# Accumulating DMAs for all weight sums, one norm step for four heads, and two K-parts in the first output projection

## The chip, the cores and the metric

The kernel runs on one core of a Trainium2 chip and computes two model blocks in one program. The metric is device time in microseconds; the time before is 1748.75 us, the median of three runs (1745.6 to 1749.56).

## The reference

512 tokens and 16 meta tokens (L = 528 rows) of width 2048 go through two blocks, all in float32. Cut to what matters:

```python
# block 1
hn   = rmsnorm(h, pre_norm_g)
proj = hn @ w_in                       # 2048 -> qa, ka, va, ga | qb, kb, vb, gb
ya   = softmax(rope(rms(q)) @ rope(rms(k)).T / sqrt(128)) @ v      # 8 heads "A", 2 kv heads
ya  *= silu(ga)
a    = softmax(q1 @ k1.T / 8 - slope*dist) - lam * softmax(q2 @ k2.T / 8 - slope*dist)
yb   = rms(a @ vb) * (1 - lambda_init) * silu(gb)                  # 8 heads "B"
h    = h + rmsnorm(concat(ya, yb) @ w_out, post_norm_g)
# block 2 (512 tokens): stick-breaking attention and a gated linear recurrence,
# each gated by silu, concatenated, projected by w_out_2 and added to h
```

## The kernel before, in words

Every float32 product is made of three TensorE passes on float32r halves (`PASSES`): a tile is cast by ScalarE to a high half and VectorE subtracts it to get the low half (`split`, lines 167 to 169). Weights come by SyncE DMAs into `wraw`, and are split into `wsp`.

Matmuls are queued on TensorE in an order that the program fixes while it is written. `run` (line 226) holds one main generator (the projections) and many side generators (the attention heads), and keeps a clock, `state["clock"]`, that adds an estimated cost for each matmul. A step that needs the result of other engines waits for a key; `post(key, ns)` (line 208) makes that key ready `ns + 300` after the clock. A side step whose keys are ready is queued ahead of the main work, and where the main generator itself waits for a key, side steps follow one another with no main work between them. What is fixed there is only the order: on the chip each matmul starts when its semaphores allow.

Block 1 goes in this order on TensorE. First K and V of attention A and its queries. Then 20 **pairs** (`PAIRS`: four pairs of gates of A, four of gates of B, then for every two B heads a Q/K pair, a V pair and a Q/K pair). A pair computes two 128-column tiles of the projection; 12 of its 16 K tiles go through `seven` (line 428), seven products of sums of weight halves with sums of input halves in place of eight, the other four K tiles through `rest`. The products are queued as 1, 4, 5, rest 6, 3, rest 6, 2, 7, rest 8, rest 8, 9; each product is 18 matmuls. The raw halves r0 to r3 of a pair are 128 x 768. `produce(p, i)` (line 356) splits the weight of product i and starts the next sum: r0 becomes w0+w1 by a VectorE add (line 373), then +w2 and +w3 by GpSimd DMAs that accumulate into SBUF (`sum_up`, line 352), and r1 becomes w1+w2 by another such DMA. GpSimd also does half of the rope of attention A (line 663), the bias table of a B head (line 882) and one step of its norm (line 964), in one queue with these DMAs.

The side steps of attention: `a_scores` (line 806) normalizes one A query head (a Square, a reduction, `rsqrt` with 12 small VectorE instructions, rope), transposes it and queues four score groups; `a_sums`/`pv_steps` (line 693) transpose the probabilities (two groups of four transposes into the one PSUM tile `ptt`, lines 705 to 711), split them into `pt` and multiply by V (`pmt`, 13 matmuls). `b_scores` (line 878) queues eight score groups of a B head through the one PSUM tile `pss`, each read by the fused add-and-minimum of line 912; `b_sums` (line 934) does its values and norm. The Q/K pair of head h may only empty product 5's bank into `qs_` when the head before it has been taken up (key `qkused`, line 1266), and the first V pair when attention A is done (key `suma`, line 1292).

After the pairs comes the first output projection O1: 512-column strips n, each summed over four K groups kg of 512; kg 3 needs the last four B heads. Strip 0 is summed over kg 0 to 2 and copied to SBUF (`to_part`), strip 1 over kg 0 to 3, then strip 0 gets kg 3; strips 2 and 3 follow by token pairs. Weights of O1 may only be loaded when `barred` is raised (line 1314), after the last pair.

Of the kernel before, what the change touches and what calls it, by code (L numbers as in the profile page):

```python
# [16 lines left out]
P = 128  # L17
# [77 lines left out]
def _sequence():  # L95


    seq = [("VA", 0)] + [("QA0", kg) for kg in range(4)] + [("QA1", kg) for kg in range(4)] + [("VA", 1)]
    seq += [("O1", 0, kg) for kg in range(3)] + [("O1", 1, kg) for kg in range(4)] + [("O1", 0, 3)]
    seq += [("O1", n, kg) for _ in range(2) for n in (2, 3) for kg in range(4)]  # L100
    seq += [("XL", b) for _ in range(2) for b in range(8)]
    seq += [("GL", b) for b in range(8)] + [("GS", b) for b in range(8)]
    for c in range(4):
        if c % 2 == 0:
            seq += [("v", c // 2, kg) for kg in range(4)]
        seq += [("qk", c, kg) for kg in (QK_LAST if c == 3 else range(4))]
    seq += [("O2", n, kg) for n in range(4) for kg in (0, 2, 3)] + [("O2", n, 1) for n in range(4)]
    return [(("KA", i), h) for h in range(2) for i in range(2)] + [(u, h) for u in seq for h in range(2)]
# [3 lines left out]
def hybrid_two_block_kernel(ctx: ExitStack, tc: tile.TileContext, wp, wq, wc, xT, xtok, par, lvec, cst, rg, pg, lruw, out):  # L112
# [92 lines left out]

    HOP = 300.0

    def post(key, ns=0.0):
        ready[key] = state["clock"] + (ns + HOP if ns else 0.0)

    def hold(key):
        ready[key] = math.inf
# [139 lines left out]
    def sum_up(p, r, q):  # L352

        pool.dma_start(pair_raw[(p, r)], wq[p, q], accum_op=ALU.add)  # L354

    def produce(p, i):


        if p >= len(PAIRS):
            return  # L360
        r = lambda k: pair_raw[(p, k)]
        if i == 1:
            pair_w[(p, "at")] = dict(zip("abcd", w_slots))
        at = pair_w[(p, "at")]
        src, place = {1: (0, "a"), 2: (0, "b"), 4: (1, "c"), 5: (3, "d"), 6: (4, "a"), 3: (0, "c"), 8: (5, "d"),
                      7: (2, "c"), 9: (0, "b")}[i]
        n = NCL * P if i in (6, 8) else WS
        slot = at[place]
        w = halves(wsp_all[:, 2 * WS * slot : 2 * WS * slot + 2 * n])
        pair_w[(p, i)] = w  # L370
        split(w[:, 0], w[:, 1], r(src))
        if i == 1:
            dve.tensor_tensor(r(0), r(0), r(1), ALU.add)
            sum_up(p, 1, 2)
        elif i == 2:
            sum_up(p, 0, 2)
        elif i == 3:
            sum_up(p, 0, 3)
        elif i == 4:
            load_raw(p, 4, raw_slot[(p, 1)])  # L380
        elif i == 5:
            load_raw(p, 5, raw_slot[(p, 3)])
        elif i == 6:
            w_slots[:] = [at["a"], at["c"], at["d"], at["b"]]
            load_raw(p + 1, 0, raw_slot[(p, 4)])
        elif i == 8:
            load_raw(p + 1, 1, raw_slot[(p, 5)])
        elif i == 7:
            load_raw(p + 1, 2, raw_slot[(p, 2)])
        elif i == 9:  # L390
            load_raw(p + 1, 3, raw_slot[(p, 0)])
# [36 lines left out]
    def seven(p, r, c0a, c0b, evac_a1, evac_b, evac_a2, after=None):  # L428
# [43 lines left out]
        if p == 0:  # L472
            yield when("x4")
        yield from product(7, 1, lambda xs, j: big[:, xs, j, HL + c0b : L], slice(c0b, HL), True, False)
        produce(p + 1, 2)
        if after:
            after()
        yield from rest(8, 2, 0, False, True, True)
        yield from rest(8, 1, c0b, True, False, True)
        yield from evac_b()  # L480
        produce(p + 1, 4)
        yield from product(9, 3, lambda xs, j: big[:, xs, KS + j, X2], allc, False, True)
        yield from evac_a2()
        produce(p + 1, 5)
# [248 lines left out]
    va = [None, None]  # L733
    lnload = [None, None]
    kb_ = [None]

    def side_norms():
        ready[("start", -1)] = 14000.0
# [67 lines left out]
    def a_scores(h, e):  # L806
        g = h // 4
        yield when(("qa", g), *([("feat", h - 1)] if h else []))
        x = qraw[:, :, (h % 4) * P : (h % 4 + 1) * P]
        act.activation(blocks(at1), x, AF.Square)  # L810
        ssq = small(4)
        dve.tensor_reduce(ssq, blocks(at1), axis=AX.X, op=ALU.add)
        rope(x, rsqrt(ssq, 4, 1.0 / P), 4, cq, sq_, at1, au)
        post(("pq", h), 14000)
        if h % 4 == 3:
            post(("qaused", g))
        yield when(("pq", h), "pmt", ("kt", 0), ("kt", 1), *([("scored", h - 2)] if h > 1 else []))
        tb = pmt()
        for t in range(NT):
            tr(tb[:, t * P : (t + 1) * P], at1[:, t * P : (t + 1) * P], ident)  # L820
        qh = T([P, 2, 512], "qq", F32R, 2)
        split(qh[:, 0], qh[:, 1], tb)
        post("pmt", 2400)
        post(("feat", h))
        post(("q", h), 3600)
        for qt in range(4):
            yield when(("q", h), "pss", 1)
            take_e(1)
            s = pst()
            qs = slice(qt * P, (qt + 1) * P)  # L830
            for pi, (a, b) in enumerate(PASSES):
                for c in range(2):
                    mm(s[:, c, :HL], qh[:, a, qs], kt_[0][:, g, b, c * HL : (c + 1) * HL], pi == 0, pi == 2)
            nm, l = small(1), small(2)
            sv = s[:, :, :HL]
            dve.tensor_reduce(nm, sv, axis=AX.XY, op=ALU.max, negate=True)  # L836
            x = et()
            act.activation(halves(x), sv, AF.Exp, bias=nm, accum_out=l[:, 0:1])  # L838
# [327 lines left out]
    def main_work():  # L1166
# [31 lines left out]
        def last_x2k1(kt):  # L1198
            if kt == KS - 1:
                post("x2k1")  # L1200
            elif kt == 11:
                for r in range(4):
                    load_raw(0, r, r)
                produce(0, 1)
                produce(0, 4)

# [2 lines left out]
        produce(0, 5)  # L1209
        yield when("xs")  # L1210
        banks = [pjt() for _ in range(4)]
        r0, r1, r2_, r3 = banks
        HR = HL - NM
        pair_no = {pair: i for i, pair in enumerate(PAIRS)}
# [48 lines left out]
        def qkb(h):  # L1263
# [14 lines left out]
                return ()  # L1278

            def after():  # L1280
                for kt in range(KS):
                    split_ready(kt)

# [32 lines left out]
        part = [ar[:, c : c + 512] for c in (2560, 4608, 5120, 5632)]  # L1316

        def o1_evac(n, from_part=False):
            c = slice(n * 512, (n + 1) * 512)

            def evac(accs):
                yield when("pgb")
                for t in accs:
                    y = accs[t]
                    if from_part:
                        y = part[t]
# [6 lines left out]
        def to_part(accs):  # L1333
            yield when(("vused", 7), ("qkused", 7))
            for t in accs:
                act.copy(part[t], accs[t])

        def o1(n, kgs, evac, toks=range(NT)):
            def slots(kg):
# [244 lines left out]
```

## Time and profile before

| | |
|---|---|
| median of 3 runs | 1748.75 us |
| the profiled execution: its own time | 1746.56 us |
| its span, first to last instruction | 1744.8 us |
| matmuls on TensorE | 10288, busy for 1691.8 us |
| VectorE, ScalarE, GpSimd busy | 1131.7, 899.3, 135.8 us |
| pairs 0 to 8, at 157 to 429 us | gates of A and B, first Q/K pair, attention A beside them |
| pairs 9 to 19, at 429 to 738 us | Q, K and V of B, attention B beside them |
| O1, from 738 us | with the last B heads up to 850 us |

In the tables of stretches, each row gives the length of a stretch, then the busy time of TensorE (PE), of its weight loads (PEld), VectorE (DVE), ScalarE (ACT) and GpSimd (POOL) with their instructions, the clock granted to TensorE as a share of full speed (PEclk), and the DMA load. In a row of waits stand the waiting instruction, what released it, the total, the times and the longest. In a timeline row stand the start and the length in microseconds, engine, line, operation, tiles and shapes, and in brackets the idle time of the engine just before it. SPq and POOLq are the DMA queues of SyncE and GpSimd.

### The profile page before, as it was taken

Reading aid. Unit: us, or ns where it says so; the run is one execution under the profiler, and the core shown is the slowest. Engines: PE = TensorE matmul, PEld = TensorE weight load, DVE = VectorE, ACT = ScalarE, POOL = GpSimd, SP = SyncE. Lnnn points to the kernel's source line nnn. Section 1 sums busy time; section 2 is a strip of 40 time slices with the busy share of each in tenths; the row PEclk is TensorE's granted clock in tenths of the full one; section 3 lists DMA queues with packets and bytes.
Section 4 is the critical chain, followed back from the end, with each engine's and each line's share of the span. In section 5 each row is a group of like instructions: output and inputs, shape, how many; then the busy total and the mean of one; then the engine's idle time right before and its main releaser. Section 6 shows DMA issues by size and latency. Waiting matters only on the chain.

```text
span 1744.8 us, 26494 instructions
## 1 busy us (share of the span) xinstructions
PE 1691.8 (97%) x10288; PEld 1504.6 (86%) x10288; DVE 1131.7 (65%) x1947; ACT 899.3 (52%) x1489; POOL 135.8 (8%) x145
## 2 busy tenths in 40 slices
PE   8999998999999998999799999999999999999998
PEld 8789988999999998978588998888888888888887
DVE  5775778877788888875458868843223564585433
ACT  6454555665566676665345548832222654565311
POOL 0101111110112111110000001100000000000000
PEclk9999999999999999999899999999999999999999
DMA  8444754656645554543368664223332222432223
GB/s 301 156 132 128 181 131 116 156 142 156 145 116 130 124 136 105 151 138 94 106 217 273 211 198 129 83 97 97 97 97 93 77 73 85 138 116 85 85 90 127
DMA packets 82668, 231.70 MB, mean 133 GB/s; under 512 B 9312, under 2 KB 15072, under 8 KB 80864
## 3 DMA queue, kind: packets, MB, share of 16 engines
q1 hardware_dynamic: 73904, 206.43, 36.9%
q0 software_dynamic: 8640, 23.60, 8.6%
q8 instruction: 80, 1.31, 0.3%
q14 instruction: 44, 0.36, 0.1%
HBM read 212.17 MB, written 17.83 MB: 132 GB/s over the span
## 4 chain that ended last, share of the span: by engine, by line
PE 77%; DVE 4%; DMA 1%; ACT 1%; issue 1%; POOL 0%; SPq 0%; ACTq 0%; DVEq 0%; POOLq 0%
PE pj L201 67%; PE pmt L201 3%; PE pss L201 3%; PE ptt L204 2%; PE bank L201 1%; DVE wsp L169 1%; PE pmt L204 1%; PE pss L204 1%; DVE e L912 0%; DMA wraw<-in_wc 0%; DMA yd<-xmisc 0%; DVE ar L960 0%; ACT wsp L168 0%; DVE pt L169 0%; DMA wraw<-in_wp 0%
## 5 line engine op out<-in xcount | busy, mean ns | idle before, releaser
L201 PE MATMUL pj<-wsp,big 128*128 128x512 f32 x3072 | 739.4, 397 | 16.5 <-ACT big L168 10.4
L201 PEld LDWEIGHTS pj<-wsp,big 128*128 128x128 f32 x3072 | 572.7, 189 | 145.5 <-ACT big L168 10.8
L201 PE MATMUL pj<-big,wsp 128*128 128x264 f32 (+3 forms) x4320 | 636.7, 304 | 9.3 <-ACT big L543 5.6
L201 PEld LDWEIGHTS pj<-big,wsp 128*128 128x128 f32 x4320 | 582.8, 189 | 46.4 <-ACT big L543 5.9
L169 DVE TENSOR_TENSOR wsp<-wraw,wsp 128x1024 fp32r<-128x1024 f32 (+3 forms) x399 | 425.0, 1068 | 300.5 <-ACT wsp L168 294.9
L168 ACT CAST wsp<-wraw 128x1024 fp32r<-128x1024 f32 (+3 forms) x399 | 366.4, 922 | 412.9 <-PE pj L201 330.2
L201 PE MATMUL pj<-x,wsp 128*128 128x264 f32 x720 | 102.1, 288 | 0.2 <-DVE wsp L169 0.2
L201 PEld LDWEIGHTS pj<-x,wsp 128*128 128x128 f32 x720 | 93.6, 190 | 0.6 <-DVE wsp L169 0.4
L354 POOL DMA_DIRECT2D wraw<-in_wq x60 | 52.7, 879 | 381.1 <-DVE wsp L169 154.9
L169 DVE TENSOR_TENSOR pt<-ptt,pt 128x512 fp32r<-128x512 f32 (+2 forms) x96 | 59.5, 619 | 30.8 <-ACT pt L168 29.5
L201 PE MATMUL pss<-kk,qq 128*128 128x264 f32 x448 | 73.7, 293 | 4.3 <-DVE sm L912 3.8
L201 PE MATMUL pmt<-pt,vv 128*128 128x256 f32 (+1 forms) x528 | 72.4, 287 | 4.9 <-DVE ptail L716 3.2
L201 PEld LDWEIGHTS pmt<-pt,vv 128*128 128x128 f32 x528 | 69.7, 196 | 7.8 <-issue 3.3
L915 ACT ACTIVATE e<-e,sm 128x528 f32<-128x528 f32 x64 | 47.2, 737 | 52.7 <-DVE sm L912 52.0
L168 ACT CAST pt<-ptt 128x512 fp32r<-128x512 f32 (+2 forms) x96 | 50.2, 523 | 40.8 <-PE ptt L204 40.5
L201 PEld LDWEIGHTS pss<-kk,qq 128*128 128x128 f32 x448 | 63.4, 193 | 7.3 <-DVE sm L912 4.6
L204 PE MATMUL ptt<-ident,e 128*128 128x128 f32 x336 | 53.2, 275 | 10.3 <-DVE pt L169 10.3
L912 DVE CUSTOM_DVE_ANT_0 e<-pss,ar 128x528 f32<-128x528 f32 x64 | 45.0, 703 | 18.4 <-PE pss L201 18.0
L204 PEld LDWEIGHTS ptt<-ident,e 128*128 128x128 f32 x336 | 40.0, 141 | 14.7 <-DVE pt L169 8.6
L201 PE MATMUL pj<-x1s,wsp 128*128 128x264 f32 x360 | 50.8, 287 | 0.0
L1120 POOL TENSOR_SCALAR_AFFINE_SELECT e<-e 128x128 f32<-128x128 f32 x32 | 12.7, 395 | 479.2 <-ACT e L1119 473.2
L838 ACT ACTIVATE e<-pss,sm 128x528 f32<-128x528 f32 x32 | 22.5, 702 | 48.3 <-DVE sm L836 48.2
(249 smaller groups left out, 1438.1 us busy)
## 6 DMA issues: line engine op xcount, KB each, us to landing
wraw<-in_wp SPq DMA_DIRECT2D x215, 512.0 KB, 3.5
wraw<-in_wq SPq DMA_DIRECT2D x80, 384.0 KB, 3.4
wraw<-in_wq POOLq DMA_DIRECT2D x60, 384.0 KB, 5.0
wraw<-in_wc SPq DMA_DIRECT2D x40, 256.0 KB, 2.7
e<-in_xT SPq DMA_DIRECT2D x28, 264.0 KB, 4.4
early<-in_xtok SPq DMA_DIRECT2D x4, 1024.0 KB, 7.2
gated<-e SPq DMA_DIRECT2D x16, 256.0 KB, 2.3
e<-yd SPq DMA_DIRECT2D x16, 256.0 KB, 3.8
```

The costliest lines, as they stand in the source:

```text
L168: act.copy(hi, src)
L169: dve.tensor_tensor(lo, src, f(hi), ALU.subtract)
L201: _queue(nc.tensor.matmul(out, lhsT, rhs, start=start, stop=stop).ins, cost)
L204: _queue(nc.tensor.transpose(out, in_, identity).ins, 110.0)
L354: pool.dma_start(pair_raw[(p, r)], wq[p, q], accum_op=ALU.add)
L838: act.activation(halves(x), sv, AF.Exp, bias=nm, accum_out=l[:, 0:1])
L912: dve.tensor_tensor_reduce(out=halves(x), in0=s[:, :, :HL], in1=halves(bias[:, b0 : b0 + L]), scale=1.0, scalar=3e38, op0=ALU.add, op1=ALU ...
L915: act.activation(x, x, AF.Exp, scale=-1.0, bias=nm, accum_out=l[:, m : m + 1])
L1120: pool.affine_select(z[:, t * P : w], z[:, t * P : w], [[-1, P]], ALU.is_gt, -1e30, base=0, channel_multiplier=1)
```

## The change

Five things are edited.

- **Weight sums.** r0 + w1 is now a DMA too (`sum_up(p, 0, 1)`), so each pair has four accumulating DMAs and no VectorE add. r1 + w2 is issued as soon as r1 of the next pair has been requested, after product 5. The split of product 4 is now made after product 7 and that of product 2 after the rests of 8; the places in `wsp` rotate in another way to suit.
- **Norms.** At heads 0 and 4 of attention A one step squares and reduces all four heads and does one `rsqrt` on 16 columns; the other heads read its result.
- **Pace.** From the first pair to the last, `post` multiplies its delays by 1.35, so the side steps are queued later.
- **First weights of O1.** In `after`, which the last Q/K pair calls, `barred` is raised and one load is emitted after product 7 of the last pair, no longer after the pair.
- **O1.** Strip 1 is also summed over kg 0 to 2 first and copied to SBUF, in the space of `x1s`; kg 3 of strip 1 and of strip 0 follow. The weights are used in the same sequence as before. Four copies and four adds come in.

```diff
-    seq += [("O1", 0, kg) for kg in range(3)] + [("O1", 1, kg) for kg in range(4)] + [("O1", 0, 3)]
+    seq += [("O1", n, kg) for n in range(2) for kg in range(3)] + [("O1", 1, 3), ("O1", 0, 3)]
...
+    pace = [1.0]
     def post(key, ns=0.0):
-        ready[key] = state["clock"] + (ns + HOP if ns else 0.0)
+        ready[key] = state["clock"] + (ns * pace[0] + HOP if ns else 0.0)
...
         if i == 1:
-            dve.tensor_tensor(r(0), r(0), r(1), ALU.add)
-            sum_up(p, 1, 2)
+            sum_up(p, 0, 1)
...
         elif i == 6:
-            w_slots[:] = [at["a"], at["c"], at["d"], at["b"]]
+            w_slots[:] = [at["a"], at["d"], at["c"], at["b"]]
             load_raw(p + 1, 0, raw_slot[(p, 4)])
         elif i == 8:
             load_raw(p + 1, 1, raw_slot[(p, 5)])
+            if p + 1 < len(PAIRS):
+                sum_up(p + 1, 1, 2)
...
         yield from product(7, 1, lambda xs, j: big[:, xs, j, HL + c0b : L], slice(c0b, HL), True, False)
-        produce(p + 1, 2)
+        produce(p + 1, 4)
...
         yield from evac_b()
-        produce(p + 1, 4)
+        produce(p + 1, 2)
         yield from product(9, 3, lambda xs, j: big[:, xs, KS + j, X2], allc, False, True)
...
-        act.activation(blocks(at1), x, AF.Square)
-        ssq = small(4)
-        dve.tensor_reduce(ssq, blocks(at1), axis=AX.X, op=ALU.add)
-        rope(x, rsqrt(ssq, 4, 1.0 / P), 4, cq, sq_, at1, au)
+        if h % 4 == 0:
+            ssq = small(16)
+            for t in range(NT):
+                sq = et(512)
+                act.activation(sq, qraw[:, t, :], AF.Square)
+                dve.tensor_reduce(ssq[:, 4 * t : 4 * t + 4], blocks(sq), axis=AX.X, op=ALU.add)
+            rnq[0] = T([P, NT, 4], "rnq", F32, 2)
+            dve.tensor_copy(flat(rnq[0]), rsqrt(ssq, 16, 1.0 / P))
+        rope(x, rnq[0][:, :, h % 4], 4, cq, sq_, at1, au)
...
         banks = [pjt() for _ in range(4)]
+        pace[0] = 1.35
...
             def after():
+                barred[0] = len(seq)
+                for _ in load_next():
+                    pass
                 for kt in range(KS):
                     split_ready(kt)
...
-        barred[0] = len(seq)
+        pace[0] = 1.0
...
-        yield from o1(0, (0, 1, 2), to_part)
-        yield from o1(1, range(4), o1_evac(1))
-        yield from o1(0, (3,), o1_evac(0, True))
+        yield from o1(0, (0, 1, 2), to_part(0))
+        yield from o1(1, (0, 1, 2), to_part(1))
+        yield from o1(1, (3,), o1_evac(1, part[1]))
+        yield from o1(0, (3,), o1_evac(0, part[0]))
```

Line numbers of the changed kernel are 3 to 20 higher than those before; the numbers in the text are those before, unless it says otherwise.

How the order of TensorE moves is seen at three places. In these rows `pj` is a bank of a pair's products, `ptt` the transposes of probabilities, `pss<-kk,qq` a score group, `pmt<-pt,vv` the values, `pmt<-ident,e` a transposed tail of 16 columns, `x_835` the input halves `x23`.

TensorE in pair 4 before, from the first transposes of a half head to the second:

```order
L204 MATMUL ptt<-ident,e 128x128 x4
L201 MATMUL pj<-big,wsp 128x248 x12
L201 MATMUL pj<-x_835,wsp 128x264 x18
L201 MATMUL pj<-big,wsp 128x264 x6
L204 MATMUL ptt<-ident,e 128x128 x4
```

And the same step in pair 4 of the changed kernel:

```order
L204 MATMUL ptt<-ident,e 128x128 x4
L201 MATMUL pj<-big,wsp 128x248 x18
L201 MATMUL pj<-x_835,wsp 128x264 x18
L201 MATMUL pj<-big,wsp 128x264 x9
L204 MATMUL ptt<-ident,e 128x128 x4
```

36 matmuls of the pair stood between the two, now 45 do.

TensorE in pair 14 before, from product 5 and rest 6 to product 3 (`x_835` in the last row):

```order
L201 MATMUL pj<-big,wsp 128x248 x30
L201 MATMUL pss<-kk,qq 128x264 x4
L204 MATMUL ptt<-ident,e 128x128 x4
L204 MATMUL pmt<-ident,e 16x128 x2
L201 MATMUL pss<-kk,qq 128x264 x4
L201 MATMUL pmt<-pt,vv 128x256 x12
L201 MATMUL pmt<-ptail,vtail_95 128x256
L201 MATMUL pss<-kk,qq 128x264 x4
L201 MATMUL pj<-x_835,wsp 128x264 x9
```

And in the changed kernel, from the last matmuls of rest 6 to the last score group ahead of product 3:

```order
L201 MATMUL pj<-big,wsp 128x248 x9
L201 MATMUL pss<-kk,qq 128x264 x4
L201 MATMUL pmt<-e,ones 128x512 x2
L201 MATMUL pss<-kk,qq 128x264 x4
L204 MATMUL ptt<-ident,e 128x128 x4
L201 MATMUL pss<-kk,qq 128x264 x8
L204 MATMUL ptt<-ident,e 128x128 x4
L204 MATMUL pmt<-ident,e 16x128 x2
L201 MATMUL pss<-kk,qq 128x264 x4
L201 MATMUL pmt<-pt,vv 128x256 x12
L201 MATMUL pmt<-ptail,vtail_95 128x256
L201 MATMUL pss<-kk,qq 128x264 x4
```

Three score groups and one set of values stood between rest 6 and product 3, with no matmul of the pair among them; now six score groups, two sets of transposes and the values do. Pair 17 has the same rows.

TensorE in pair 9 before, from product 5 and rest 6 into product 3 and the second rest 6:

```order
L201 MATMUL pj<-big,wsp 128x264 x30
L201 MATMUL pj<-x_835,wsp 128x264 x12
L201 MATMUL pss<-kk,qq 128x264 x4
L201 MATMUL pj<-x_835,wsp 128x264 x6
L201 MATMUL pj<-big,wsp 128x264 x12
```

And in the changed kernel, from the last matmuls of rest 6 to product 3:

```order
L201 MATMUL pj<-big,wsp 128x264 x9
L204 MATMUL ptt<-ident,e 128x128 x4
L204 MATMUL pmt<-ident,e 16x128 x2
L201 MATMUL pss<-kk,qq 128x264 x6
L201 MATMUL pmt<-pt,vv 128x256 x12
L201 MATMUL pmt<-ptail,vtail_96 128x256
L204 MATMUL ptt<-ident,e 128x128 x8
L204 MATMUL pmt<-ident,e 16x128 x2
L201 MATMUL pss<-kk,qq 128x264 x8
L201 MATMUL pmt<-pt,vv 128x256 x12
L201 MATMUL pmt<-ptail,vtail_96 128x256
L201 MATMUL pj<-x_835,wsp 128x264 x18
```

Attention A ended in pair 8 before; now its last head ends here, ahead of product 3, again with no matmul of the pair in between.

More of the change, by code (lines that the diff above doesn't have):

```diff
@@ L735, in hybrid_two_block_kernel @@
     kb_ = [None]
+    rnq = [None]
     def side_norms():
@@ L1203, in last_x2k1 @@
                     load_raw(0, r, r)
+                sum_up(0, 1, 2)
                 produce(0, 1)
@@ L1313, in main_work, with o1_evac @@
             yield from qkb(h + 1)
-        barred[0] = len(seq)
-        part = [ar[:, c : c + 512] for c in (2560, 4608, 5120, 5632)]
-        def o1_evac(n, from_part=False):
+        pace[0] = 1.0
+        more = T([P, 2048], "x1s")
+        part = [[ar[:, c : c + 512] for c in (2560, 4608, 5120, 5632)],
+                [more[:, c : c + 512] for c in range(0, 2048, 512)]]
+        def o1_evac(n, from_part=None):
             c = slice(n * 512, (n + 1) * 512)
@@ L1325, in evac @@
                     if from_part:
-                        y = part[t]
+                        y = from_part[t]
                         dve.tensor_tensor(y, accs[t], y, ALU.add)
@@ L1331, in o1_evac, with to_part, evac @@
             return evac
[L1333 to L1336, printed above, removed]
+        def to_part(n):
+            def evac(accs):
+                yield when(("vused", 7), ("qkused", 7))
+                for t in accs:
+                    act.copy(part[n][t], accs[t])
+            return evac
         def o1(n, kgs, evac, toks=range(NT)):
```

## The prediction

> **What bounds the kernel now.** I read the page's head first, then busy time by stretches, then the list of TensorE's waits in each stretch, then the timeline at the longest waits.
>
> ```profile
> span 1744.8 us, 26494 instructions
> PE 1691.8 (97%) x10288; PEld 1504.6 (86%) x10288; DVE 1131.7 (65%) x1947; ACT 899.3 (52%) x1489; POOL 135.8 (8%) x145
> 157.00:439.00 282.00, 268.29 (x2218) 264.93 (x2217) 213.93 (x417) 158.00 (x286) 38.73 (x42) 0.99 0.59 147
> 439.00:739.00 300.00, 291.52 (x2366) 288.34 (x2364) 255.54 (x491) 198.41 (x377) 51.52 (x41) 0.98 0.53 128
> 739.00:860.00 121.00, 102.99 (x493) 84.98 (x493) 67.93 (x120) 61.32 (x115) 8.27 (x4) 0.92 0.34 111
> 860.00:1745.00 885.00, 880.37 (x4390) 737.80 (x4389) 493.89 (x698) 398.99 (x590) 25.14 (x40) 1.00 0.39 124
> ```
>
> TensorE is the bound. The change leaves its matmuls alone, so it can only move what TensorE loses: idle time, and busy time at a lowered clock. I count the loss of a stretch as length minus PE busy, plus (1 - PEclk) times PE busy. The first pairs lose 13.7 + 0.01 x 268 = 16.4 us; pairs 9 to 19 lose 8.5 + 0.02 x 292 = 14.3; O1 loses 18.0 + 0.08 x 103 = 26.2. The last 885 us, which the change doesn't touch, lose under 5. So some 57 us are in play. The waits of the three stretches, in order:
>
> ```profile
> PE ptt L204 <- DVE pt L169: 10.3, 5, 3.0
> PE pmt L201 <- DVE qq L169: 1.7, 2, 1.2
> PE pss L201 <- DVE sm L912: 3.8, 3, 3.1
> PE pmt L201 <- DVE ptail L716: 2.8, 2, 1.4
> PE pj L201 <- DVE wsp L169: 1.8, 2, 1.7
> PE pj L201 <- ACT big L168: 10.4, 1, 10.4
> PE pj L201 <- DVE wsp L169: 6.2, 1, 6.2
> ```
>
> In the first stretch the second transposes of a half head wait for `ptt` to be read; in the second score groups and values wait in two places; in O1 TensorE waits for the first weights (6.2) and for the last gated head (10.4).
>
> **The first pairs: norms and pace.** Two of the five `ptt` waits look like this one in pair 4:
>
> ```profile
> 288.46 0.69 DVE L812 TENSOR_REDUCE sm<-ar 128x4 f32<-128x512 f32 x1 [0.46 <-ACT ar L810]
> 289.93 0.60 PE L204 MATMUL ptt<-ident,e 128*128 128x128 f32 x4
> 291.74 2.39 PE L201 MATMUL pj<-x,wsp 128*128 128x264 f32 x18
> 292.15 0.16 DVE L180 SCALAR_TENSOR_TENSOR sm<-sm 128x4 f32<-128x4 f32 x1
> 297.12 0.69 DVE L169 TENSOR_TENSOR pt<-ptt,pt 128x512 fp32r<-128x512 f32 x1 [0.35 <-ACT pt L168]
> 297.87 0.65 PE L204 MATMUL ptt<-ident,e 128*128 128x128 f32 x4 [3.00 <-DVE pt L169]
> 249.08 1.12 PE L204 MATMUL ptt<-ident,e 128*128 128x128 f32 x4 [2.96 <-DVE pt L169]
> ```
>
> The reduction and the 12 small steps of `rsqrt` hold VectorE from 288.46 to 292.31, all but one split of 0.95, so some 2.9 us; the rope and a row maximum follow, and `pt` is read only at 297.81. From the first transposes (290.53) that is 7.3 us, while 36 matmuls lay between. The new step takes the 2.9 away at six of eight heads, and nine more matmuls lie between (9 x 0.13, from the 18 in 2.39), so 1.2 more cover: 3.0 - 2.9 - 1.2 is below zero, the wait goes, and nothing is late behind it. The wait at 249.08 has no norm ahead of it but the evacuation of a gate; it keeps 2.96 - 1.2 = 1.8. Heads 4 to 7 now get four reductions (2.8 us) and one chain (2.4) in a row, once; I give that 1.5. With 1.2 for the rest, 4.5 of 16.4 stay: **-12**, between -6 (only the two waits with a norm, with their slow clock) and -16 (all). The VectorE adds that go are worth nothing by themselves:
>
> ```profile
> L373 DVE TENSOR_TENSOR wraw<-wraw x20: 949/957/960, 147.4 to 702.4; 128x768 f32<-128x768 f32 x20
> DMA to landing us min/median/max: 4.6/5.0/7.4
> ```
>
> 20 x 0.957 = 19 us leave an engine that is not the bound; they only shorten its queue. The second row is of the accumulating DMAs, which take their place.
>
> **The price of the pace: attention piles up ahead of product 3.** Product 3 of a Q/K or V pair is queued behind an evacuation that waits for attention. With delays 1.35 times as long attention is behind there, and what is left is queued in one piece with nothing of the pair between. The trace has such a piece, of pair 17:
>
> ```profile
> 655.25 0.65 PE L201 MATMUL pss<-kk,qq 128*128 128x264 f32 x4
> 657.96 0.76 DVE L928 SCALAR_TENSOR_TENSOR e<-e,sm 128x528 f32<-128x528 f32 x1
> 659.24 0.70 DVE L912 CUSTOM_DVE_ANT_0 e<-pss,ar 128x528 f32<-128x528 f32 x1
> 660.00 0.76 PE L201 MATMUL pss<-kk,qq 128*128 128x264 f32 x4 [3.08 <-DVE sm L912]
> 663.48 0.41 DVE L716 TENSOR_TENSOR ptail<-pmt,ptail 16x256 fp32r<-16x256 f32 x1
> 664.03 2.90 PE L201 MATMUL pmt<-pt,vv 128*128 128x256 f32 x12 [1.42 <-DVE ptail L716]
> 711.79 1.58 PE L201 MATMUL pmt<-pt,vv 128*128 128x256 f32 x12
> 656.00:667.00 11.00, 6.35 (x37) 5.57 (x36) 8.43 (x19) 6.61 (x14) 0.89 (x1) 0.77 0.48 121
> ```
>
> Each score group (0.65) must be read by line 912 (0.70) before the next may write `pss`, and VectorE is busy with other things. After the waits the clock is down: 12 value matmuls take 2.90 against 1.58 elsewhere. The stretch loses 4.65 + 0.23 x 6.35 = 6.1 us. The Trainium skill, page "TensorE: Matmul & The Clock Gate", section "Part 1: The HAM clock gate", says the clock halves after an idle window of about 3.4 us; the trace lowers it after waits of 3.08 and 1.42, so smaller gaps also pay. If only gaps beyond that window paid, the sum below would be some 4 us lower, with a loss of 6.5 in each of the long pieces.
>
> In pairs 14 and 17 six score groups now stand together, with a second set of transposes. Low bound: 4 us each, about what pair 14 costs today (14.3 less 6.1 and 1.8 leaves 6 for it and the rest). High bound: 12, twice pair 17's 6.1. By hand: five times 0.65 + 0.70 and a hop of 0.1 between groups is 7.3, in which 3 us of transposes and values fit; the three line-928 steps (0.76) and the norm steps of the head before stand between the reads of line 912, and the values still wait for `ptail` and run slow. I take 8.5. Pairs 13 and 16 get a short piece, two score groups around the values: 1 each. With 0.5 for `wsp` the second stretch loses 19.5 against 14.3: **+5**, between -4 and +13.
>
> Pair 9 is new: the last A head ends there. Its price comes from the same kind of steps:
>
> ```profile
> L838 ACT ACTIVATE e<-pss,sm 128x528 f32<-128x528 f32 x29 | 20.4, 702 | 46.9 <-DVE sm L836 46.8
> 828.42 0.59 ACT L168 CAST pt<-ptt 128x512 fp32r<-128x512 f32 x1 [2.63 <-PE ptt L204]
> 829.04 0.69 DVE L169 TENSOR_TENSOR pt<-ptt,pt 128x512 fp32r<-128x512 f32 x1 [1.99 <-ACT pt L168]
> 829.76 0.42 DVE L716 TENSOR_TENSOR ptail<-pmt,ptail 16x256 fp32r<-16x256 f32 x1
> 831.00 1.58 PE L201 MATMUL pmt<-pt,vv 128*128 128x256 f32 x12
> ```
>
> The first values wait for `pt` and `ptail` behind transposes (0.59 + 0.69 + 0.42 less one score group of 0.9): about 1.2 with hops. The eight transposes in a row need `ptt` read in their middle: 0.59 + 0.69 and a hop, 1.4. The two B score groups wait for `pt`, `ptail` and line 912: 1.6. With 1.3 for the clock: **+5.5**, between +3 and +9.
>
> **O1.**
>
> ```profile
> 743.94 2.35 DVE L169 TENSOR_TENSOR wsp<-wraw,wsp 128x1024 fp32r<-128x1024 f32 x2
> 745.21 1.22 PE L201 MATMUL pj<-wsp,big 128*128 128x512 f32 x2 [6.18 <-DVE wsp L169]
> 738.00:752.00 14.00, 7.82 (x30) 6.19 (x29) 12.43 (x22) 8.37 (x15) 1.77 (x1) 0.76 0.62 213
> ```
>
> The low half of the first weights is made at 743.94, behind the splits of gated heads. Its place in `wsp` reaches into that of product 9; in the new rotation product 9's weight lies elsewhere and the load is emitted one product earlier, ahead of two of these splits. The loss is 6.2 + 0.24 x 7.8 = 8.1; I leave 1.5, as VectorE still has five 0.69-us jobs ahead of it beside the 6 us of rest 8 and product 9: **-6.5**, between -8 and -3.
>
> At the end of kg 0 to 2 the last B head now has its second transposes behind the 288th matmul, where before only values were left. So `pt` and `ptail` (0.59 + 0.69 + 0.42, and hops) come on the path to the 10.4-us wait, less cover: **+1.5**, between 0 and +3. The four copies and four adds run beside matmuls. The order of units doesn't change, so the wait itself stays.
>
> **Sums by DMA.** r0 now passes three DMAs between splits, each 4.6 to 7.4 us. The tight link is split 2 (after the second rest 8), a DMA, split 3, product 3. On TensorE product 9, products 1, 4 and 5 and a rest lie between: 84 matmuls, 84 x 0.13 = 11 us, and attention. Two splits take 2 x 1.9 (cast, then 0.95), the DMA 5.0: 8.8. It fits with 2 us to spare, in most pairs more; GpSimd also has rope and bias in that queue, and ScalarE stands still where a split comes too early. **+1**, between 0 and +8.
>
> The sum: -12 + 5 + 5.5 - 6.5 + 1.5 + 1 = -5.5. Against the profiled execution's own 1746.56 that is 1741; it lay 2.2 under the median, so against 1748.75 it is **1743**.
>
> **Rivals.**
> - *The pieces are cheap* (0.25): VectorE, relieved of adds and norms, reads each score group at once, as in most rows of line 912. Then pairs 14 and 17 cost 5 each and pair 9 costs 3, the second stretch stands at -2, and the sum is -12 - 2 + 3 - 6.5 + 1.5 = -16: 1733. For it speaks that VectorE has 44 us free in the 300; against it the 3.08 above.
> - *The pieces are dear, slower* (0.13): VectorE is late for two groups in each long piece, 12 us each, 4 in pairs 13 and 16, 9 in pair 9: -12 + 18 + 9 - 6.5 + 2 + 1 = +11, 1760. It ends above the old time once the long pieces cost over 11 us each.
> - *The sums land late, slower* (0.07): GpSimd's queue stands behind a bias table or a rope, product 3 waits 0.6 us in each of 20 pairs, 12 in all: 1754. Page "DMA: Bandwidth & Descriptors" of the Trainium skill, section "SWDGE vs HWDGE vs iDMA", names a cause, VectorE locking GpSimd out of the memory where it writes descriptors; nothing in the rows above shows it.
> - *Nothing is left* (0.10): the pace only moves waits from the first stretch into the second, and the sum is within 3 of zero: 1748.
>
> **How the numbers follow.** The forecast has 0.45, mostly -11 to 0. A measurement of this kernel tells 0.2% (3.5 us) from no change. Faster by more: 0.34 of the forecast's 0.45, all 0.25 of the first rival and 0.01 of the last, 0.60. Within: 0.08 + 0.09 = 0.17. Slower: 0.03 + 0.13 + 0.07 = 0.23. The range 1731 to 1757 takes in the forecast, most of the first rival and the late sums; outside are most of the dear pieces and the far end of the cheap.
>
> **What would show it.** Right: `ptt` waits of 157 to 439 under 5 us in all; no wait over 2 at the start of O1; long waits on line 912's successor and `ptail` in the pieces of pairs 9, 14 and 17, with a clock near 0.8. Wrong: no loss there, or more than 11 us in a piece; waits of `pj` on `wsp` behind GpSimd DMAs all through the pairs; a `ptt` loss as before, though no norm stands ahead of it.

## The result, and the profile after

The changed kernel took 1776.07 us (median of four, 1770.61 to 1777.05) against 1747.32 for the kernel before beside it: the ratio is 1.0157, with a 95% interval of 1.0132 to 1.0183. By the ratio it is 27 us slower, by the medians 29. The forecast said 1743, its range ended at 1757, and the dearest rival stood at 1760.

The profiled execution is the fastest of the four, 1770.61 us with a span of 1768.8. First the busy time by stretches of the kernel after: pairs 0 to 8, pair 9, pairs 10 to 19, O1, the rest. The columns are those of the table before; the loss of a row is again its length less PE busy, plus (1 - PEclk) times PE busy.

```profile
157.00:417.00 260.00, 248.22 (x2061) 245.11 (x2061) 183.02 (x331) 141.31 (x254) 42.12 (x45) 1.00 0.69 165
417.00:459.00 42.00, 36.49 (x278) 35.29 (x277) 27.16 (x52) 23.80 (x45) 4.54 (x6) 0.92 0.48 107
459.00:765.00 306.00, 283.09 (x2224) 277.54 (x2223) 235.37 (x452) 187.68 (x354) 57.40 (x49) 0.96 0.57 131
765.00:886.00 121.00, 106.39 (x530) 87.90 (x529) 74.05 (x131) 68.05 (x130) 7.79 (x4) 0.94 0.34 107
886.00:1769.00 883.00, 878.71 (x4383) 736.39 (x4381) 492.39 (x697) 398.14 (x588) 25.36 (x40) 1.00 0.39 124
```

| | forecast: loss that stays | after |
|---|---|---|
| pairs 0 to 8 | 16.4 - 12 = 4.4 | 11.8 |
| pair 9 | 5.5 | 5.5 + 0.08 x 36.5 = 8.4 |
| pairs 10 to 19 | 19.5 | 22.9 + 0.04 x 283 = 34.2 |
| O1 | 26.2 - 6.5 + 1.5 = 21.2 | 14.6 + 0.06 x 106 = 21.0 |

O1 is as forecast. The first pairs keep 7 us more than forecast, and pairs 9 to 19 keep 18 more: 25 of the 30 us that lie between the forecast for a profiled execution (1741) and this one. PEclk is given in hundredths, so a row of 300 us is uncertain by 1.5; the other 5 us don't show in this count.

The second stage is where the change loses. The same view for five short stretches of the kernel after, in pairs 9, 14, 16, 17 and 19:

```profile
434.00:445.00 11.00, 7.22 (x40) 6.55 (x39) 4.44 (x10) 5.54 (x12) 0.00 (x0) 0.69 0.17 37
573.00:591.00 18.00, 11.54 (x57) 9.79 (x56) 12.96 (x30) 11.50 (x26) 2.43 (x3) 0.72 0.38 89
639.00:650.00 11.00, 6.70 (x42) 6.26 (x41) 6.74 (x16) 7.73 (x16) 1.76 (x2) 0.84 0.48 108
674.00:691.00 17.00, 11.02 (x59) 9.27 (x59) 11.98 (x28) 11.15 (x24) 2.18 (x2) 0.80 0.41 95
739.00:752.00 13.00, 8.51 (x48) 8.06 (x46) 7.70 (x18) 8.83 (x18) 2.45 (x2) 0.74 0.38 91
```

They lose 6.0, 9.7, 5.4, 8.2 and 6.7 us, and each lies ahead of a product 3. Counted in thirteen stretches with borders at the pieces, so that the rounding of the clock weighs less, the stage loses 39.9 us and not 43. All but 0.8 of that lies in six pieces: 7.7 in pair 9 (from 429), 0.9 in pair 13, then 10.0, 5.5, 8.3 and 6.8 in pairs 14, 16, 17 and 19. TensorE's waits in pairs 9 to 19 of the kernel after (us in total, times, longest):

```profile
PE pmt L201 <- DVE ptail L719: 11.1, 6, 3.2
PE pss L201 <- DVE sm L921: 7.1, 9, 1.4
PE ptt L204 <- DVE e L937: 6.2, 2, 3.4
PE ptt L204 <- DVE pt L169: 2.4, 1, 2.4
```

Line 921 is what was line 912, 719 what was 716, and 937 what was 928. Waits for `ptail` and for line 921 are the ones that the forecast named for the pieces. The third row is not: in pairs 14 and 17 the second transposes wait 3.4 and 2.9 us for the probabilities themselves, which line 937 makes, and that is the longest wait of each of these two pieces. In the first pairs the waits of `ptt` are gone, and others stand in their place:

```profile
PE pj L201 <- ACT xmisc L457: 4.0, 4, 1.4
PE pmt L201 <- DVE qq L169: 2.7, 2, 2.1
PE pj L201 <- DVE e L1241: 2.4, 1, 2.4
```

What changed most is seen on no list of TensorE. It is ScalarE's wait for a weight, pairs 0 to 19, in the kernel before and then in the kernel after:

```profile
ACT wsp L168 <- DMA wraw<-in_wq: 9.6, 5, 3.3
```

```profile
ACT wsp L168 <- DMA wraw<-in_wq: 50.1, 20, 4.1
```

A cast that opens a split now stands still 20 times for these weights, with all that is queued behind it on ScalarE. For the weights of the rests, `in_wc`, its waits fell from 7.7 to 0.8 us.

### The profile page after: what moved, and what is told of

It reads as the page before. It is cut to its first block, busy times and chain, and to the rows that moved or that the text cites. A ratio compares the mean times of both kernels' runs of the same rounds, so it can differ in the third digit from the quotient of the medians.

```text
span 1768.8 us, 26488 instructions
## 1 busy us (share of the span) xinstructions
PE 1700.2 (96%) x10288; PEld 1509.4 (85%) x10288; DVE 1110.1 (63%) x1861; ACT 902.2 (51%) x1493; POOL 151.6 (9%) x165
## 4 chain that ended last, share of the span: by engine, by line
PE 56%; DVE 1%; DMA 1%; ACT 0%; issue 0%; DVEq 0%; ACTq 0%; SPq 0%
PE pj L201 51%; PE pmt L201 2%; PE pss L201 1%; PE bank L201 1%; PE ptt L204 1%; PE pmt L204 0%; PE pss L204 0%; DMA wraw<-in_wp 0%; DMA wraw<-in_wq 0%; DVE wsp L169 0%; DMA yd<-xmisc 0%; DMA e<-yd 0%; DVE pt L169 0%; ACT wsp L168 0%; DVE ptail L719 0%
## 5 line engine op out<-in xcount | busy, mean ns | idle before, releaser
L201 PE MATMUL pj<-wsp,big 128*128 128x512 f32 x3072 | 738.0, 397 | 10.2 <-ACT big L168 10.2
L201 PEld LDWEIGHTS pj<-wsp,big 128*128 128x128 f32 x3072 | 571.8, 189 | 138.4 <-ACT big L168 10.6
L356 POOL DMA_DIRECT2D wraw<-in_wq x80 | 70.0, 888 | 467.1 <-DVE wsp L169 294.3
L201 PE MATMUL pmt<-pt,vv 128*128 128x256 f32 (+1 forms) x528 | 75.9, 296 | 16.8 <-DVE ptail L719 14.1
L201 PEld LDWEIGHTS pj<-x1s,wsp 128*128 128x128 f32 x360 | 45.8, 188 | 2.9 <-DVE e L1241 2.6
```

The source lines that it names most:

```text
L201: _queue(nc.tensor.matmul(out, lhsT, rhs, start=start, stop=stop).ins, cost)
```

## The experiments

Two theories were set against each other. **A, the factor:** with 1.35 attention piles up ahead of product 3, and that is the loss. **B, the sums:** with all sums by DMA the casts wait, and what is queued behind them is late. Ratios are to the kernel before on the same chip, with their 95% interval.

**The factor alone undone.**

```diff
-        pace[0] = 1.35
+        pace[0] = 1.0
```

> The changed kernel with the factor on the delays back at 1.0; sums, norms, early load and O1 as changed. Theory A (the factor: attention piled up ahead of product 3 is the loss): the serial pieces of pairs 9, 13, 16 and 19 go, those of 14 and 17 shrink to their old size, 9.4 + 1.6 + 11.9 + 6.7 + 10.5 + 8.0 = 48 us of loss become some 17, and the first pairs get 3 to 6 back: 1776 - 31 + 5 = 1750. Theory B (the sums: three accumulating DMAs in a row make the casts of ScalarE wait, 20 waits and 50 us against 5 waits and 9.6 before, and what is queued behind them is late): the casts still wait, so at least half of the loss of 28 us stays wherever attention now stands: 1762 or more.

Measured: 1748.05, ratio 1.0015 (1.0004 to 1.0026). The time of theory A: in this kernel's order the pieces of pairs 9, 13, 16 and 19 are gone, and those of 14 and 17, back at three score groups, lose 2.0 and 7.1 us. But it is not below the kernel before, though it has the norms and the early load.

**The sums alone undone, and both undone.** The lines of the weight sums, the order of products 2 and 4 and the places in `wsp` go back to those of before. In both kernels the early load of O1 then overwrites the place that product 9 of the last pair reads, so that product works on another weight's data.

```diff
-            sum_up(p, 0, 1)
+            dve.tensor_tensor(r(0), r(0), r(1), ALU.add)
+            sum_up(p, 1, 2)
...
-            w_slots[:] = [at["a"], at["d"], at["c"], at["b"]]
+            w_slots[:] = [at["a"], at["c"], at["d"], at["b"]]
...
-            if p + 1 < len(PAIRS):
-                sum_up(p + 1, 1, 2)
```

> The changed kernel with the sums of before (one VectorE add, two accumulating DMAs behind it, the order of products 2 and 4 and the places of before); the factor 1.35 stays. Theory A (the factor): the pieces stay, 1776 less 0 to 4: 1772 to 1776. Theory B (the sums): ScalarE's waits for the sums fall from 50 us to about 10; the pieces of pairs 16 and 19 (6.7 and 8.0 us) fall to the 1.6 of pair 13, and the first pairs gain the 8 us that the forecast missed: 1776 - 11 - 8 = 1757, or below.

> Both undone: sums of before and factor 1.0, with the norms of four heads, the early load and the new K order of O1. If factor and sums each cost for themselves, this lies below before: the norms of four heads take 3 to 6 us of the first pairs away, the early load 6 at the start of O1, the K order gives 1 to 3 back: 1738 to 1744. If it lies at 1747 or above, norms or O1 lose too, and the loss isn't only in factor and sums.

Measured: with the factor at 1.35, 1771.51, ratio 1.0151 (1.0136 to 1.0166), no different from the changed kernel; with both undone 1732.87, ratio 0.9936 (0.9916 to 0.9956). The first of these two is against theory B as the cause of the 27 us. The second shows that the sums do cost, where the factor is 1.0. The stretches of pairs 0 to 8 and 9 to 19 in the kernel with 1.35 and the sums of before:

```profile
157.00:416.00 259.00, 251.13 (x2081) 248.69 (x2080) 193.59 (x342) 143.42 (x256) 35.05 (x37) 0.99 0.60 153
416.00:767.00 351.00, 323.57 (x2498) 316.11 (x2497) 275.06 (x518) 212.19 (x400) 53.38 (x44) 0.94 0.48 119
```

It loses 10.4 in the first pairs and 27.4 + 0.06 x 324 = 46.8 in the second stage. Counted in short stretches that is 43.4, and the same six pieces lose 39.6 of it, where they lose 39.1 in the changed kernel: with either kind of sums, the factor's price stands in these pieces.

**The factor in the gate pairs only.**

```diff
         for h in range(0, 8, 2):
+            pace[0] = 1.0
             yield from qkb(h)
```

> The changed kernel with the factor 1.35 in the gate pairs 0 to 7 only, and 1.0 from pair 8 on. Theory A (the factor, in the B pairs alone): the pieces of pairs 13 to 19 fall to what they cost before (39 us of loss to 16), pair 9 may keep its piece: 1776 - 23 = 1753, or 1745 without the piece of pair 9. Theory B (the sums): casts wait for the sums as before, and the losses stay over 15 above before: 1762 or more.

Measured: 1750.15, ratio 1.0023 (1.0008 to 1.0037). Theory A again: what 1.35 costs, it costs from pair 8 on. In the gate pairs it is worth nothing: factor 1.0 throughout gave 1.0015.

**A version of the parts that pay.** The kernel with both undone, with places so turned that no weight is overwritten.

```diff
-    w_slots = [0, 2, 1, 3]
+    w_slots = [0, 2, 3, 1]
...
                 produce(0, 1)
-                produce(0, 4)
+                produce(0, 5)
...
+        produce(0, 4)
         produce(0, 2)
-        produce(0, 5)
```

> Sums of before and factor 1.0, with the norms of four heads, the early load and the new K order of O1; the starting places of the weights are turned so that the early load of O1 doesn't meet product 9 of the last pair (pair 0 makes weight 5 ahead of weight 4). If the time of the third experiment wasn't owed to its misplaced weight: 1732 to 1735. If it was, the early load waits for product 9 again: 1739 to 1742.

Measured: 1734.98, ratio 0.9923 (0.9907 to 0.9938): the fastest kernel of this study, 13 us below the kernel before. Its two stretches:

```profile
157.00:423.00 266.00, 257.99 (x2135) 254.92 (x2134) 198.06 (x356) 148.86 (x273) 35.26 (x38) 0.99 0.60 148
423.00:732.00 309.00, 297.91 (x2438) 294.76 (x2438) 264.20 (x502) 204.96 (x388) 51.59 (x42) 0.99 0.54 129
```

They lose 10.6 and 14.1. Beside the kernel with 1.35 and the same sums, the first stage is equal and the second is 33 us better. So we have four corners:

| | factor 1.0 | factor 1.35 |
|---|---|---|
| sums of before | 0.9923 (0.9907 to 0.9938) | 1.0151 (1.0136 to 1.0166) |
| sums by DMA | 1.0015 (1.0004 to 1.0026) | 1.0157 (1.0132 to 1.0183) |

The corner with 1.35 and the sums of before has the overwritten place; its exact counterpart at 1.0 gave 0.9936, inside the interval of the first corner. The factor costs 2.3% (40 us) with the sums of before and 1.4% (25 us) with the new ones. The sums cost 0.9% (16 us) at factor 1.0, and nothing that can be measured at 1.35.

**The norms alone.** The kernel before with `a_scores` of after.

```diff
-        act.activation(blocks(at1), x, AF.Square)
-        ssq = small(4)
-        dve.tensor_reduce(ssq, blocks(at1), axis=AX.X, op=ALU.add)
-        rope(x, rsqrt(ssq, 4, 1.0 / P), 4, cq, sq_, at1, au)
+        if h % 4 == 0:
+            ssq = small(16)
...
+        rope(x, rnq[0][:, :, h % 4], 4, cq, sq_, at1, au)
```

> The kernel before with the norms of four heads in one step, and nothing else. If the norms bring what the gate pairs gained in the third experiment (loss 22.1 to 16.4): 1745.6 - 6 = 1740. If the gain there came from the delays or the order around them: 1744 to 1747. Forecast's step (the wait behind a norm goes, 12 us together with the longer gap): 1738 to 1740.

Measured: 1737.55, ratio 0.9943 (0.9929 to 0.9957), 10 us faster. Nearly all of the fifth kernel's gain is here. Pairs 0 to 8 and 9 to 19:

```profile
157.00:422.00 265.00, 258.58 (x2137) 256.23 (x2136) 198.19 (x357) 150.82 (x275) 35.84 (x39) 0.99 0.61 151
422.00:728.00 306.00, 297.10 (x2444) 294.07 (x2443) 265.18 (x504) 204.73 (x388) 51.60 (x42) 1.00 0.54 129
```

The first pairs lose 9.0, where the kernel before lost about 16. The second stage loses 8.9 against 14.3, although no norm of A lies in it; where that comes from wasn't followed up.

**One sum left out, and the order around the sums.** Three kernels at factor 1.0 ask what it is in the sums that costs. The first does not issue the DMA r0 + w1, the second exchanges two loads, the third puts that DMA in the place of VectorE's add and leaves the order of before.

```diff
         if i == 1:
-            sum_up(p, 0, 1)
+            pass
```

> The changed kernel with the factor at 1.0 and the first of the three sums into the first raw weight left out (the DMA is not issued; that product's data lack a term), so the order of products 2 and 4 and the places stay as changed. If the time goes into the third DMA of the chain (ScalarE's casts wait for it): the casts' waits fall from 39 us to about 10 and the time to 1735 to 1738. If it goes into the order of products 2 and 4 and the other places: 1745 to 1748.

Measured: 1743.79, ratio 0.9982 (0.997 to 0.9995). Between the two theories: some 6 of the 16 us are that DMA, 10 come with the new order and places.

```diff
-            load_raw(p + 1, 0, raw_slot[(p, 4)])
+            load_raw(p + 1, 1, raw_slot[(p, 4)])
...
-            load_raw(p + 1, 1, raw_slot[(p, 5)])
+            load_raw(p + 1, 0, raw_slot[(p, 5)])
```

> The changed kernel with the factor at 1.0, and the loads of raw weights 1 and 0 of the next pair exchanged: weight 1, into which an accumulating DMA adds, is loaded two splits earlier. Theory B1 (the cost of the sums is the split of product 4, now ahead of product 8's matmuls, that waits for load and accumulation of weight 1): ScalarE's waits for that split fall from 24 us to under 8 and the time from 1748 to 1738 to 1743. Theory B2 (the third accumulating DMA on weight 0 is the cost): no gain, or slower since weight 0 now comes later: 1748 to 1755.

Measured: 1744.32, ratio 0.9981 (0.9967 to 0.9996), a gain of 0.3% and less than B1 forecast. In the trace the casts of product 4 no longer wait; those of product 1, whose weight is now loaded later, wait 18.6 us in their place.

```diff
-            dve.tensor_tensor(r(0), r(0), r(1), ALU.add)
+            sum_up(p, 0, 1)
             sum_up(p, 1, 2)
```

> The fifth kernel (1735) with its one VectorE add replaced by an accumulating DMA, in the order and the places of before, so that only the engine of that sum changes. Theory B1 (the new order costs, a DMA more doesn't): 1735 to 1738. Theory B2 (three accumulating DMAs in a row on weight 0): the split of product 2, right behind product 7, waits 2 to 4 us in most of 20 pairs, and the time rises to 1745 or more.

Measured: 1785.69, ratio 1.0219 (1.0203 to 1.0236). In each of 20 pairs one VectorE add of 0.96 us became a DMA, and against the fifth kernel this one loses 51 us. The new order isn't where the cost of that DMA comes from: it is what makes it bearable. An example from pair 11 of this kernel, by the timeline:

```profile
515.60 1.75 POOL L356 DMA_DIRECT2D wraw<-in_wq  x2 [5.90 <-DVE sm L920]
524.24 0.83 ACT L168 CAST wsp<-wraw 128x768 fp32r<-128x768 f32 x1 [6.31 <-DMA wraw<-in_wq]
525.10 0.96 DVE L169 TENSOR_TENSOR wsp<-wraw,wsp 128x768 fp32r<-128x768 f32 x1 [6.64 <-ACT wsp L168]
526.74 1.25 PE L201 MATMUL pss<-kk,qq 128*128 128x264 f32 x4 [2.11 <-DVE sm L920]
```

GpSimd issues two accumulating DMAs 0.6 us apart, which land at 520.4 and 524.1. ScalarE comes to the cast of a split and waits 6.31, until the later one is in; VectorE stands 6.64 behind the cast; the score group that VectorE should read in that time is read late, and TensorE waits 2.11 for it. ScalarE's wait for the weights of `in_wq` in pairs 0 to 19, in the order fifth kernel, sum left out, loads exchanged, factor 1.0 only, DMA in the old order:

```profile
ACT wsp L168 <- DMA wraw<-in_wq: 17.2, 8, 6.1
```

```profile
ACT wsp L168 <- DMA wraw<-in_wq: 26.4, 12, 4.7
```

```profile
ACT wsp L168 <- DMA wraw<-in_wq: 32.7, 16, 4.4
```

```profile
ACT wsp L168 <- DMA wraw<-in_wq: 36.9, 17, 4.4
```

```profile
ACT wsp L168 <- DMA wraw<-in_wq: 82.5, 19, 9.5
```

Their times are 1735.0, 1743.8, 1744.3, 1748.1 and 1785.7. From the first to the last, 65.3 us more of waiting cost 50.7 us, 0.78 each; the three between lie within 3 us of that line (1742.2, 1747.1 and 1750.4). All five do the same work on TensorE. This is a relation among five kernels, and the last of them sets the slope. With the waits for `in_wc` added (5.3, 0.9, 1.0, 3.1 and 10.2 us) it is 0.72, and the second kernel lies 5 us off. The kernel with the norms alone waits 9.1 us for `in_wq` and takes 1737.6, 9 more than the line; so a microsecond of this wait has no fixed price.

**The K order of O1.** The fifth kernel with the K order of before.

```diff
-        yield from o1(1, (0, 1, 2), to_part(1))
-        yield from o1(1, (3,), o1_evac(1, part[1]))
+        yield from o1(1, range(4), o1_evac(1))
```

> The fifth kernel with the K order of before in O1: only norms and early load are left of the change. If the K order costs what the forecast gave it (the last transposes come nearer to the end of the wait: 0 to 3 us), this is 0 to 3 faster than the fifth; if the K order is what shortens O1 (25.2 of loss before, 17.3 in the third experiment), it is 3 to 8 slower.

Measured: 1736.31, ratio 0.9931 (0.9915 to 0.9947), against 0.9923 (0.9907 to 0.9938) with it. The two can't be told apart. The early load can't be told from the noise either: this kernel is the norms and the early load, and the norms alone gave 0.9943 (0.9929 to 0.9957). In the trace the early load does what it is for: with the norms alone TensorE waits 6.1 us for the first weights of O1, and here that wait is gone.

**Other factors.** The fifth kernel with 0.85 and with 1.15.

```diff
-        pace[0] = 1.0
+        pace[0] = 0.85
```

> The fifth kernel (1735) with factor 0.85. In its order of instructions no piece of attention stands ahead of product 3 in pairs 14 and 17. If those pieces are the price (4.9 and 7.1 us of loss there in the fifth): 1735 - 12, less up to 6 for shorter gaps between steps: 1723 to 1729. If attention costs the same wherever it is queued, since VectorE and ScalarE need the time: 1733 to 1740.

> The fifth kernel (1735) with factor 1.15. In its order of instructions six score groups with two sets of transposes and the values stand ahead of product 3 in pairs 14 and 17, as with 1.35, but pairs 9, 13, 16 and 19 have no piece. By the price of such a piece (11 each with 1.35, against 4.9 and 7.1 in the fifth): 1735 + 10 = 1745. If the loss with 1.35 grows with the delays all over and not with the pieces, a bit under half of the 36 us between factors 1.0 and 1.35: 1751.

Measured: 1746.73 with 0.85, ratio 0.9994 (0.9984 to 1.0004), and 1754.47 with 1.15, ratio 1.0033 (1.0021 to 1.0045). In both, pairs 14 and 17 did what the pieces said. Their stretches, in the kernel with 0.85 and no piece there, then in the fifth (1.0), with 1.15, and in the changed kernel (1.35):

```profile
566.00:596.00 30.00, 29.68 (x244) 29.20 (x243) 25.78 (x51) 23.39 (x48) 5.58 (x4) 1.00 0.46 109
657.00:687.00 30.00, 29.33 (x242) 28.79 (x241) 26.57 (x54) 22.66 (x46) 5.12 (x4) 1.00 0.55 118
```

```profile
555.00:587.00 32.00, 28.34 (x233) 27.59 (x232) 29.05 (x58) 22.29 (x44) 5.21 (x5) 1.00 0.45 114
641.00:677.00 36.00, 31.47 (x247) 30.74 (x247) 30.45 (x59) 24.10 (x48) 6.44 (x5) 0.95 0.41 104
```

```profile
565.00:605.00 40.00, 34.67 (x261) 33.42 (x260) 32.22 (x66) 26.63 (x53) 7.35 (x5) 0.91 0.40 94
658.00:699.00 41.00, 35.58 (x261) 34.31 (x260) 32.18 (x67) 26.75 (x53) 7.34 (x5) 0.88 0.39 94
```

```profile
562.00:605.00 43.00, 36.54 (x265) 34.73 (x264) 33.52 (x68) 27.26 (x55) 7.92 (x7) 0.88 0.44 100
664.00:705.00 41.00, 35.02 (x260) 33.21 (x259) 31.55 (x65) 26.84 (x55) 7.48 (x7) 0.92 0.45 103
```

The two pairs lose 1.0, 9.8, 18.1 and 19.6 us: without a piece there is hardly a loss, and it doubles from a piece of three score groups (1.0; 1.7 of its 9.8 is a wait for a weight ahead of the piece) to one of six (1.15 and 1.35). The totals missed what the pieces let expect, by 18 us or more with 0.85 and by some 9 with 1.15, since the factor moves other things too. With 0.85 the first pairs lose 11.8 + 0.01 x 259 = 14.4, against 10.6, and TensorE waits 4.1 us for a score group to be read right behind pair 19. With 1.15 the first pairs lose 17.1 + 0.04 x 264 = 27.7, and the rows of pair 5 show one reason (by the timeline):

```profile
321.21 0.62 ACT L168 CAST wsp<-wraw 128x512 fp32r<-128x512 f32 x1 [4.84 <-DMA wraw<-in_wc]
323.49 0.38 ACT L456 COPY xmisc<-pj 128x264 f32<-128x264 f32 x1
323.91 0.71 PEld L201 LDWEIGHTS pj<-big,wsp 128*128 128x128 f32 x3 [3.48 <-ACT xmisc L456]
```

Here no sum is at work, only a plain load that comes late: the cast of a split waits 4.84 for it, the copy of product 1 stands behind the cast, and the next product waits 3.48 for the copy. It is the mechanism of the sums once more, set off by the factor. Why the load itself came late there wasn't tried.

## Why the prediction was wrong, point by point

- *First pairs, -12.* The norms: mechanism right. By themselves they bring 10 us, 7 of it in the first pairs (loss 15.8 to 9.0). The longer gap was to carry the rest; it carried nothing. With the same sums the first stage loses 10.4 at 1.35 and 10.6 at 1.0. At 1.35 the waits of `ptt` did go, but waits of products for a copy of ScalarE and for an evacuation came in: 4.0 and 2.4 us in the changed kernel, 4.7 and 2.4 with the sums of before. So they aren't owed to the new sums, and 11.8 stayed.
- *Pieces of pairs 14 and 17, 8.5 each.* The size is right, 9.7 and 8.2, the make-up only in part. The sum had score groups late at line 912 and slow values behind `ptail`. Those waits are 1.6 and 1.3 us in each piece; the largest, 3.4 and 2.9, is that of the second transposes for line 937, which the forecast had only as work that holds VectorE. That the sum came out is partly luck.
- *"Pairs 13 and 16 get a short piece, two score groups around the values: 1 each."* This is the step that failed most. Pair 19 has one too and was overlooked, and pairs 16 and 19 cost 5.4 and 6.7, together 12 us where the forecast had 1. The rows of the changed kernel in pairs 13 and 16, then those of the kernel with 1.35 and the sums of before in the same two pairs:

```profile
541.14 0.60 PE L204 MATMUL ptt<-ident,e 128*128 128x128 f32 x4
541.72 2.30 PE L201 MATMUL pj<-big,wsp 128*128 128x248 f32 x18
545.41 1.71 PE L201 MATMUL pmt<-pt,vv 128*128 128x256 f32 x12 [0.91 <-DVE ptail L719]
...
638.77 0.60 PE L204 MATMUL ptt<-ident,e 128*128 128x128 f32 x4
638.89 1.60 ACT L168 CAST wsp<-wraw 128x768 fp32r<-128x768 f32 x2 [3.83 <-DMA wraw<-in_wq]
639.34 0.93 PE L201 MATMUL pj<-big,wsp 128*128 128x248 f32 x6
645.32 2.73 PE L201 MATMUL pmt<-pt,vv 128*128 128x256 f32 x12 [3.17 <-DVE ptail L719]
```

```profile
540.43 0.60 PE L204 MATMUL ptt<-ident,e 128*128 128x128 f32 x4
540.82 1.35 ACT L168 CAST wsp<-wraw 128x512 fp32r<-128x512 f32 x2 [2.90 <-DMA wraw<-in_wc]
541.00 2.64 PE L201 MATMUL pj<-big,wsp 128*128 128x248 f32 x18
547.09 2.17 PE L201 MATMUL pmt<-pt,vv 128*128 128x256 f32 x12 [2.97 <-DVE ptail L718]
...
641.85 0.60 PE L204 MATMUL ptt<-ident,e 128*128 128x128 f32 x4
642.42 0.94 PE L201 MATMUL pj<-big,wsp 128*128 128x248 f32 x6
645.84 2.00 PE L201 MATMUL pmt<-pt,vv 128*128 128x256 f32 x12 [2.00 <-DVE ptail L718]
```

  The forecast counted score groups. What sets the wait is the chain from the transposes to the values (the cast of `pt` and two VectorE steps) and the matmuls that cover it. The chain takes 4.0 to 4.3 us from the start of the transposes (541.14 to 545.41, and 641.85 to 645.84). Where ScalarE is held in between by a cast that waits for a DMA, it takes 6.5 to 6.7 (638.77 to 645.32, and 540.43 to 547.09); in pair 19 of the changed kernel, which has the order of pair 16, 6.8. The cover is 18 matmuls of the pair in pair 13 and 6 in pairs 16 and 19, in both kernels. So thin cover alone gives a wait of 2.0, a late DMA behind good cover 3.0, and both together 3.2 and another 1.1 ahead of a score group. The late DMA need not be a sum: in pair 13 with the sums of before it is a plain load. The three short pieces lose 13.2 us in the changed kernel and 12.0 with the sums of before.
- *Pair 9, +5.5.* Measured 8.4, inside the bounds of 3 to 9.
- *O1, -6.5 and +1.5.* Right in the profile (21.0 against 21.2): the wait of 6.2 at its start is gone, and values wait 2.5 for `ptail` where before they didn't. As a difference in the time it can't be resolved.
- *"The tight link is split 2 ... It fits with 2 us to spare. +1."* Wrong at factor 1.0, by 15 us. That link was counted on TensorE, and it nearly fits: with the factor alone undone, the casts of product 3 wait some 3 us in all. Of the 36.9 us that casts wait there, some 24 stand at the split of product 4 and 9 at that of product 2, on ScalarE, where a cast that waits for a DMA holds the queue. The sentence on it ("ScalarE stands still where a split comes too early") was there, without a price. At 1.35 the sums cost nothing more: with the sums of before, casts wait 24 us for weights of `in_wq` there and 18 for those of `in_wc`, 42 together against 51 in the changed kernel. That this is why the two costs don't add is likely, and wasn't tried.
- *The rivals.* "The pieces are dear" came nearest. Its losses for pairs 9 to 19 add up to 41.5, against 42.6 in the table, though by luck: it had the long pieces at 12, too dear, and short ones of 4 in two pairs, where two of the three reached 5.4 and 6.7. Its 1760 was too low in part because it kept the -12 of the first pairs. "The sums land late" has its sign at factor 1.0, where the sums cost 16 us against its 12, but it looked for TensorE waiting for a weight, 0.6 in each pair, where the wait was ScalarE's.

## What to carry to other kernels

Price a later operand on each in-order queue that will wait for it: in the same order a DMA in place of a 0.96-us add cost 51 us of the kernel, with 65 us more in which ScalarE's casts stood waiting, while the add lay on an engine with time to spare. Where side work is queued without main work between, count the matmuls between each result's producer and its reader, in every place the new order has, and look at what the engines in between may be held by; a piece that looks short can have the shortest cover. And separate a bundle before judging it: here one part (the norms) was worth 10 us, and two others took 25 to 40 and up to 16.

## What the runs showed of the hardware

Accumulating DMAs of 384 KB land late when one is issued close behind another. Times to landing, minimum, median and maximum, of all 80 in the kernel with the DMA in the old order:

```profile
DMA to landing us min/median/max: 4.6/5.3/9.8
```

The 12 that start within 3 us of the one before took 6.0, 7.0 and 9.8; the 44 with no other within 6 us took 4.6, 5.0 and 7.4. The Trainium skill, page "DMA: Bandwidth & Descriptors", section "Anatomy of one DMA — SWDGE (gpsimd) path", fits a DMA of GpSimd's at 2.0 us plus its bytes over 436e3; as an estimate that is 2.9 for this size. No accumulating one in this kernel took under 4.6.

The clock fell after waits shorter than expected. The stretch at 434 has 0.69, and its waits are 2.4, 1.4 and 1.4; the 12 value matmuls behind the wait of 3.17 took 2.73, where 1.58 is usual. The Trainium skill, page "TensorE: Matmul & The Clock Gate", section "Part 1: The HAM clock gate", gives an idle window of about 3.4 us for the drop. If that is read as one unbroken wait, these rows don't agree: waits of 1.4 to 2.4 us close together lowered it as well.
